# The dilated attention layer with its tokens ordered by residue modulo 4, and 64x64 class blocks for two of its three groups

## The chip, the core and the metric

The kernel runs on one core of one Trainium2 chip. The metric is the device time of one launch in microseconds (us): the kernel before takes 2082.92 us, the median of three runs (2081.38 to 2082.97). TensorE is called PE below, VectorE DVE, ScalarE ACT, GpSimd POOL, and SyncE, whose queue issues most DMA transfers, SP.

## The reference, cut to what matters

The program is a trunk of four layers on 256 tokens of width 1024, all in float32. Each layer has a token mixer, a cross-attention into 256 memory tokens and a squared-ReLU MLP. The mixer of layer 1, the second of the four, is a dilated attention with 16 heads of 64 features:

```
DIL_GROUPS = ((128, 1), (512, 4), (2048, 16))          # (window, dilation)
qkv = (x @ w_qkv).reshape(b, s, n_groups, 3, DIL_HEADS, DIL_HEAD_DIM)
# group (win, dil): query t attends to t, t-dil, ..., t-win (causal), with a T5 bias by distance
logits = q . k * 64**-0.5 + bias
o, lse = softmax(logits) @ v, log-sum-exp(logits)      # per group, per head
wts = softmax(stack(lses), axis=0)                      # over the three groups
o = einsum('gbsh,gbshe->bshe', wts, stack(outs)) @ w_out
x = layer_norm(alpha * x + o)
```

The mean over the groups, weighted by their softmax denominators, equals one softmax over the keys of all three groups together, and that is how both kernels compute it. With 256 tokens, a query of the second group (dilation 4) meets only keys of its own residue modulo 4, and one of the third group (dilation 16) only keys of its own residue modulo 16.

## The kernel before, in words

A large matrix product is split in two: each float32 operand becomes a rounded part `h` and a remainder `l`, and three products (h times h, h times l, l times h) add up in PSUM. `chunk` (lines 129 to 139) fetches 512 KB of a weight into one of 3 buffers `ws`; ACT casts it to `wh` (L137), DVE subtracts to get `wl` (L138); `wh` and `wl` have 9 buffers each. `xth` and `xtl` hold the tokens, transposed, with features on partitions (`to_xt`, which PE's transposes at L211, ACT's cast at L151 and DVE's subtraction at L152 make).

The dilated layer works by pairs of heads, 8 pairs. A query or key projection for one pair and one group is a unit `qk_unit` (L628, 24 matmuls of 256 columns, 6 such units to a pair); a value projection for four heads and one group is 48 matmuls of 256 columns (L193, 3 such units to two pairs). The first three value units have a planned order: token tile 0 of all three, then token tile 1 (`v_units`).

For each head, `scores` multiplies queries and keys in full float32, which PE runs as two passes for one instruction. For each of the three groups there is a 256-column product for query tile 1 (L677) and a 128-column one for query tile 0 (L679). `softmax` adds the bias and takes the maximum on DVE (L657), exponentiates on ACT (L663), and normalizes on DVE (L665), in two calls of 768 and 384 columns. Keys that the group's pattern leaves out have a bias of -1e30, so that all 256 or 128 keys of each group are worked on. `flip` transposes the nine 128x128 blocks of probabilities of a head (L692) and copies them from PSUM (L694). `values` multiplies them with the values of both heads of the pair (L704), each head to its own half of the output partitions. The bias comes from a table in DRAM (`dil_table`), read once per head into `hks` with one DMA (L672). At the end `project` multiplies with `w_out` (L169) and `norm` normalizes.

The order of the instructions on each engine is set by the program order of these functions and by a scheduler in the tile framework, which moves an instruction ahead of others of its engine when it expects its operands earlier. Semaphores wait at run time, and each engine works its own list in order. PSUM has 4 buffers `psA`, 2 `psB` and 2 `psT` of one bank each.

Of the kernel before, what the change touches and what calls it, by code (L numbers as in the profile page):

```python
# [11 lines left out]
F32 = mybir.dt.float32  # L12
# [7 lines left out]
P = 128  # L20
D = 1024
# [17 lines left out]
TW = 384  # L39
# [44 lines left out]
class Trunk:  # L84
# [70 lines left out]
    def gemm_tok(self, xt, t, ws, ps, k0=0, first=True, last=True):  # L155
# [6 lines left out]
        if last:  # L162
            steps = steps[:-TAIL] + [(k, (j,)) for j in every for k in range(n - TAIL, n)]
# [20 lines left out]
    def gemm_unit(self, xt, unit, ps, tiles=(0, 1)):  # L184
# [3 lines left out]
        for m in tiles:  # L188
# [25 lines left out]
    def to_xt(self, xt, src, t):  # L214
        xh, xl = xt
        for q in range(2):
            pt = self.transposes([src[:, (4 * q + i) * P:(4 * q + i + 1) * P] for i in range(4)])
            self.split(xh[:, 4 * q:4 * q + 4, t * P:(t + 1) * P], xl[:, 4 * q:4 * q + 4, t * P:(t + 1) * P],
                       pt.rearrange("p (a b) -> p a b", a=4))
# [31 lines left out]
    def norm(self, t, ps, gb, xt):  # L251
# [16 lines left out]
        if xt is not None:  # L268
            self.to_xt(xt, x, t)
# [114 lines left out]
    def mlp(self, layer, xt, xt_out):  # L384
# [46 lines left out]
        for t in range(NT):  # L431
            for u in range(NU - skew, NU):
                down(u, t)
            self.norm(t, acc[t], gb, xt_out)
# [154 lines left out]
    def dil_table(self, pool):  # L589


        nc, t_ = self.nc, self.t
        G = len(DIL)
# [3 lines left out]
        oh = self.sb.tile([P, G, TW], F32, name="onehot", tag="kt", bufs=2)  # L597
        nc.sync.dma_start(oh[:BUCKETS + 1], t_["rel_onehot"])
        tab = self.dr.tile([G, DH, TW], F32, name="reltab")
        for g in range(G):  # L600
            ps = self.T()
            nc.tensor.matmul(ps[:DH, :TW], rb, oh[:BUCKETS + 1, g, :], start=True, stop=True)
            sb = self.g2()
            nc.scalar.copy(out=sb[:DH, :TW], in_=ps[:DH, :TW])
            nc.sync.dma_start(tab[g], sb[:DH, :TW])
        return tab

    def dilated(self, layer, j, xt, xt_out):
        nc, v, t_ = self.nc, self.nc.vector, self.t
        G = len(DIL)  # L610
        gb = self.load_gb(layer, 0)
# [4 lines left out]
        hks = self.sb.tile([P, 2, 4, S], F32, name="hks", tag="kt", bufs=2)  # L616
        sbs = self.sb.tile([P, 2, 1024], F32, name="sbs", tag="vt", bufs=2)
        qk, vv, pr, pts = {}, {}, {}, {}
        oxt = self.xt()

        def qk_unit(hp, g, c):

            c0 = (g * 3 + c) * D + hp * P
            hi, lo = self.chunk(w[:, c0:c0 + P].rearrange("(k p) n -> p k n", p=P), (KC, P))
# [4 lines left out]
            o = qk[hp, g, c] = dp.tile([P, S], F32, name="qk", bufs=12)  # L629
# [5 lines left out]
        def v_units(hq, gs):  # L635

            us = [self.colunit(w, (g * 3 + 2) * D + hq * 256) for g in gs]
            ps = [self.A() if len(gs) > 1 else self.B() for _ in gs]
            for m in range(NT):
                for u, p_ in zip(us, ps):  # L640
                    self.gemm_unit(xt, u, p_, (m,))
            for g, p_ in zip(gs, ps):
                o = vv[hq, g] = dp.tile([P, NT, 256], F32, name="vv", bufs=5)
                nc.scalar.copy(out=o, in_=p_.rearrange("p (a b) -> p a b", a=2))

        def rev(hk, g0, n, top, w_):
            a = hk[:, g0:g0 + n, top:top + 1]
            return bass.AP(tensor=a.tensor, offset=a.offset,
                           ap=[list(a.ap[0]), [S, n], [-1, w_]])

        def softmax(sv, parts, n):

            mx = None
            o = 0
            for ps, bi, k in parts:
                m2 = self.sm.tile([P, 1], F32, name="dmx", tag="dmx", bufs=4)
                v.tensor_tensor_reduce(out=sv[:, o:o + k], in0=ps, in1=bi, scale=1.0,  # L657
# [671 lines left out]
```

## Time and profile before

| what | before |
|---|---|
| median of three runs | 2082.92 us (2081.38 to 2082.97) |
| the profiled execution's own time | 2083.81 us |
| its span, first to last instruction | 2082.0 us |
| mean granted clock of TensorE | 0.971 of full speed |
| PE busy | 1973.5 us (95% of the span) |
| DVE busy | 1314.8 us (63%) |
| ACT busy | 994.3 us (48%) |
| first value matmul of the dilated layer | 463.06 us |
| first scores of the layer | 509.23 us |
| scores of the last pair begin | 750.52 us |
| normalization of its first token tile begins | 774.16 us |

Times inside a run are counted from the first instruction. A row of the timeline gives start, length, engine, line, operation, output and inputs, shapes and count; what stands in brackets is the idle time of the engine before it and what ended it. A matmul's length is its latency, and successive ones overlap, so the distance from start to start is what one costs. In the chain of waits each row is a start, a length and the work that the end of the program hung on at that time.

### The profile page before, as it was taken

Reading aid. Unit: us, or ns where it says so; the run is one execution under the profiler, and the core shown is the slowest. Engines: PE = TensorE matmul, PEld = TensorE weight load, DVE = VectorE, ACT = ScalarE, POOL = GpSimd, SP = SyncE. Lnnn points to the kernel's source line nnn. Section 1 sums busy time; section 2 is a strip of 40 time slices with the busy share of each in tenths; the row PEclk is TensorE's granted clock in tenths of the full one; section 3 lists DMA queues with packets and bytes.
Section 4 is the critical chain, followed back from the end, with each engine's and each line's share of the span. In section 5 each row is a group of like instructions: output and inputs, shape, how many; then the busy total and the mean of one; then the engine's idle time right before and its main releaser. Section 6 shows DMA issues by size and latency. Waiting matters only on the chain.

```text
span 2082.0 us, 32815 instructions
## 1 busy us (share of the span) xinstructions
PE 1973.5 (95%) x12949; PEld 1744.4 (84%) x12949; DVE 1314.8 (63%) x2516; ACT 994.3 (48%) x1548; POOL 265.1 (13%) x160
## 2 busy tenths in 40 slices
PE   7999999999999999999999989989999898999998
PEld 7998789978989987798889878767898787877996
DVE  3986575464554557655486578776654499657554
ACT  4545455544444434365435543334655355545552
POOL 6960000000000000000021221100000663000000
PEclk8999999999999999999999989999999999999999
DMA  6644456657666625376646243334665441445762
GB/s 225 203 152 143 134 172 214 191 164 185 156 152 149 166 76 182 128 224 194 189 134 212 82 130 99 122 112 131 212 203 183 159 148 52 138 135 164 220 184 79
DMA packets 260409, 327.83 MB, mean 157 GB/s; under 512 B 25333, under 2 KB 220669, under 8 KB 260256
## 3 DMA queue, kind: packets, MB, share of 16 engines
q1 hardware_dynamic: 260256, 325.75, 51.6%
q8 instruction: 101, 1.65, 0.3%
q14 instruction: 52, 0.43, 0.1%
HBM read 318.81 MB, written 6.89 MB: 156 GB/s over the span
## 4 chain that ended last, share of the span: by engine, by line
PE 69%; DVE 15%; DMA 6%; ACT 4%; issue 4%; POOL 1%; SPq 0%; DVEq 0%; ACTq 0%; POOLq 0%
PE psA L169 24%; PE psB L181 20%; PE psB L628 6%; PE psB L193 5%; DVE g L519 3%; DVE wl L138 3%; PE psT L211 3%; ACT wh L137 2%; DMA ws<-in_m_w_dram 2%; PE psB L358 2%; PE psA L193 1%; PE psA L677 1%; DVE bnst L261 1%; DMA ws<-in_a_w_in_dram 1%; DVE psA L519 1%
## 5 line engine op out<-in xcount | busy, mean ns | idle before, releaser
L137 ACT CAST wh<-ws 128x1024 fp32r<-128x1024 f32 x546 | 571.3, 1050 | 709.3 <-PE psA L169 174.1
L138 DVE TENSOR_TENSOR wl<-ws,wh 128x1024 fp32r<-128x1024 f32 (+1 forms) x462 | 568.4, 1234 | 402.4 <-ACT wh L137 394.6
L181 PE MATMUL psB<-xth,wh 128*128 128x256 f32 x1280 | 369.4, 289 | 7.6 <-ACT xth L151 3.7
L181 PE MATMUL psB<-xth,wl 128*128 128x256 f32 x1280 | 367.3, 287 | 7.7 <-DVE wl L138 7.7
L181 PE MATMUL psB<-xtl,wh 128*128 128x256 f32 x1280 | 367.1, 287 | 0.0
L181 PEld LDWEIGHTS psB<-xth,wh 128*128 128x128 f32 x1280 | 250.2, 196 | 12.0 <-ACT xth L151 4.1
L138 POOL TENSOR_TENSOR wl<-ws,wh 128x1024 fp32r<-128x1024 f32 x84 | 211.1, 2536 | 376.8 <-ACT wh L137 364.1
L181 PEld LDWEIGHTS psB<-xth,wl 128*128 128x128 f32 x1280 | 250.0, 195 | 8.8 <-DVE wl L138 8.6
L181 PEld LDWEIGHTS psB<-xtl,wh 128*128 128x128 f32 x1280 | 250.0, 195 | 2.3 <-issue 0.2
L169 PE MATMUL psA<-wh,xth 128*128 128x512 f32 x512 | 185.8, 406 | 1.4 <-ACT xth L151 0.9
L169 PE MATMUL psA<-wl,xth 128*128 128x512 f32 x512 | 181.8, 399 | 0.0
L169 PE MATMUL psA<-wh,xtl 128*128 128x512 f32 x512 | 180.4, 398 | 0.0
L169 PE MATMUL psA<-wh,hth 128*128 128x512 f32 x512 | 163.7, 396 | 0.0
L169 PE MATMUL psA<-wh,htl 128*128 128x512 f32 x512 | 163.3, 395 | 0.0
L169 PE MATMUL psA<-wl,hth 128*128 128x512 f32 x512 | 162.2, 393 | 0.0
L519 DVE SCALAR_TENSOR_TENSOR psA<-chp,ccols,psA 128x256 f32<-128x256 f32 x280 | 119.1, 481 | 2.9 <-PE psA L503 0.4
L628 PE MATMUL psB<-xth,wh 128*128 128x256 f32 x384 | 112.6, 293 | 6.1 <-ACT qk L631 4.3
L169 PEld LDWEIGHTS psA<-wh,xth 128*128 128x128 f32 x512 | 97.7, 192 | 23.6 <-ACT xth L151 5.0
L169 PEld LDWEIGHTS psA<-wl,hth 128*128 128x128 f32 x512 | 96.5, 188 | 23.0
L169 PEld LDWEIGHTS psA<-wh,htl 128*128 128x128 f32 x512 | 96.2, 188 | 22.0
L828 POOL MEMSET rH<- 128x512 f32 x1 | 0.5, 526 | 894.6 <-DVE bnst L261 894.6
L169 PEld LDWEIGHTS psA<-wl,xth 128*128 128x128 f32 x512 | 97.5, 191 | 19.4
(321 smaller groups left out, 3612.5 us busy)
## 6 DMA issues: line engine op xcount, KB each, us to landing
ws<-in_m_w_dram SPq DMA_DIRECT2D x256, 512.0 KB, 4.0
ws<-in_b_w_qkv_dram SPq DMA_DIRECT2D x72, 512.0 KB, 3.9
ws<-in_x_w_kv_dram SPq DMA_DIRECT2D x64, 512.0 KB, 3.5
ws<-in_a_w_in_dram SPq DMA_DIRECT2D x32, 512.0 KB, 3.4
ws<-in_x_w_q_dram SPq DMA_DIRECT2D x32, 512.0 KB, 4.1
ws<-in_x_w_out_dram SPq DMA_DIRECT2D x32, 512.0 KB, 3.5
ws<-in_c_w_rkv_dram SPq DMA_DIRECT2D x24, 512.0 KB, 4.4
ws<-in_a_w_out_dram SPq DMA_DIRECT2D x16, 512.0 KB, 3.2
```

Of the source, the lines that this page charges most:

```text
L137: nc.scalar.copy(out=h[:rows], in_=f[:rows])
L138: self.lo_eng.tensor_tensor(l[:rows], f[:rows], h.bitcast(F32)[:rows], op=OP.subtract)
L169: nc.tensor.matmul(ps[j], l, r[:, j * 512:(j + 1) * 512], start=first and k == 0 and i == 0, stop=last and k == n - 1 and i == 2)
L181: nc.tensor.matmul(ps[:, c * S + toks.start:c * S + toks.stop], l, r, start=k == 0 and i == 0, stop=k == KC - 1 and i == 2)
L193: nc.tensor.matmul(ps[:, m * 256:(m + 1) * 256], l, r[:, k % 4, :], start=k == 0 and i == 0, stop=k == KC - 1 and i == 2)
L211: self.pe_last = self.nc.tensor.transpose(pt[:, i * P:(i + 1) * P], b, self.ident).ins
L261: v.bn_stats(st[:, j, :], xs)
L358: nc.tensor.matmul(op[:, c * S:(c + 1) * S], vt[:, m, (2 * h + c) * P:(2 * h + c + 1) * P], pT[:, m, :], start=m == 0, stop=m == 1)
L519: v.scalar_tensor_tensor(dst[:, o], hp[:, c, k:k + S], dwc(k, cc), src[:, o], op0=OP.mult, op1=OP.add)
L628: nc.tensor.matmul(ps, l[:, k, :], r[:, k, :], start=k == 0 and i == 0, stop=k == KC - 1 and i == 2)
L677: nc.tensor.matmul(s1[g // 2][:, (g % 2) * S:(g % 2 + 1) * S], q[g][r, P:], k[g][r, :], start=True, stop=True)
L828: nc.gpsimd.memset(H, 0.0)
```

## The change

The tokens of the dilated layer are put in a new order: by residue modulo 4, so that 64 tokens of class 0 come first, then class 1, 2 and 3. The MLP before the layer writes its transposed result in that order (`to_xt` with `classes`), and the layer's own output is written back in the old order (`back` in `values`), so that nothing else sees it.

In the second and third group a query then needs only the 64 keys of its own class. For each head and tile of 128 queries, which is two classes, `scores` now makes one product with all 256 keys for the first group and four products of 64x64 for the other two. A query's logits are 256 + 64 + 64 = 384 numbers in one PSUM bank, and one softmax of 384 columns per head and token tile takes the place of the calls of 768 and 384 columns per head. The third group's values and scores of odd classes are stored in the other half of the partitions, so that one transpose and one product with the values of 128 rows serve both groups: two small copies and two DMAs from ACT's queue per four heads arrange that (`v_unit`). Bias rows are read in four DMAs per pair in place of two.

The order of the work is new too. Weights are fetched up to three items ahead (`step`). The four softmaxes of a pair are issued one after each of the next pair's first four items, then its transposes and values. The last pair's softmaxes stand beside the first seven eighths of the output projection for token tile 0. The value units come one after the other, not by token tile.

```
-        oh = self.sb.tile([P, G, TW], F32, name="onehot", tag="kt", bufs=2)
+        oh = self.sb.tile([P, 1024], F32, name="onehot", tag="kt", bufs=2)
-        for g in range(G):
+        for g in range(2):
...
+            if classes:
+                o = [a[:, k, :].rearrange("p k (a i) -> p k a i", a=NC)[:, :, :, t * n:(t + 1) * n] for a in xt]
+                self.split(*o, pt.rearrange("p (k i a) -> p k a i", k=4, a=NC))
...
+        def v_unit(hq, g, unit):
+            ps = self.B()
+            self.gemm_unit(xt, unit, ps)
...
+            if g == 1:
+                for e in range(2):
+                    nc.scalar.copy(out=vs[hq][half(e), :, e, :], in_=ps[half(e)])
+            else:
+                o = dp.tile([P, NT, 256], F32, name="v2", bufs=1)
+                nc.scalar.copy(out=o, in_=ps)
+                for e in range(2):
+                    nc.scalar.dma_start(vs[hq][half(1 - e), :, e, :], o[half(e)])
...
+        def scores(hp):
+            hk = hks[:, hp % 2]
+            bias(hp + 1)
+            hs = (2 * hp, 2 * hp + 1)
+            ps = {(h, t): self.A() for h in hs for t in range(NT)}
+            for t in range(NT):
+                for h in hs:
+                    nc.tensor.matmul(ps[h, t][:, :S], qk[hp, 0, 0][row(h), t * P:(t + 1) * P], qk[hp, 0, 1][row(h), :],
+                                     start=True, stop=True)
+            for t in range(NT):
+                for b in range(2):
+                    for e in range(2):
+                        o = slice(t * P + SI * e, t * P + SI * e + SI)
+                        for h in hs:
+                            q, k = (qk[hp, 1 + (b ^ e), c] for c in range(2))
+                            nc.tensor.matmul(ps[h, t][half(e), S + SI * b:S + SI * b + SI], q[row(h), o], k[row(h), o],
+                                             start=True, stop=True)
+            def softmax(h, t):
...
+                v.tensor_tensor_reduce(out=sv[:, :S], in0=p_[:, :S], in1=along(b0, -1, (-NC, SI), NC), scale=1.0,
+                                       scalar=-3e38, op0=OP.add, op1=OP.max, accum_out=m1)
+                v.tensor_tensor_reduce(out=sv[:, S:S + X1], in0=p_[:, S:S + X1], in1=along(b1, 1, (-2, SI), 2), scale=1.0,
+                                       scalar=m1, op0=OP.add, op1=OP.max, accum_out=m2)
...
+        def flips():
+            for n in range(3):
+                if n < 2:
+                    src = [svs[:, n, t, b * P:(b + 1) * P] for b in range(2) for t in range(NT)]
+                else:
+                    src = [svs[:, h, t, S:S + X1] for h in range(2) for t in range(NT)]
+                pt = self.transposes(src)
+                o = self.g2()
+                (v.tensor_copy if n == 1 else nc.scalar.copy)(out=o, in_=pt)
...
+        def values(hp, pts, op):
+            *p0, p1 = pts
+            for b in range(2):
+                for h in hs:
+                    nc.tensor.matmul(op[row(h), :S], v0[h // 4][:, b, f(h)], p0[h % 2][:, b * S:(b + 1) * S],
+                                     start=b == 0, stop=False)
+            for a in range(NC):
+                for h in hs:
+                    o = slice(SI * a, SI * a + SI)
+                    nc.tensor.matmul(op[row(h), o], vs[h // 4][:, a // 2, a % 2, f(h)],
+                                     p1[:, h % 2 * S + SI * a:h % 2 * S + SI * a + SI], start=False, stop=a == NC - 1)
...
+        bias(0)
+        for _ in items(0):
+            step()
+        for hp in range(HP):
+            soft = scores(hp)
+            if hp < HP - 1:
+                for _ in items(hp + 1):
+                    step()
+                    if soft:
+                        soft.pop(0)()
+                values(hp, flips(), self.B())
+        wo = t_["b_w_out"][j]
+        ws = [self.rows(wo, k) for k in range(HP - 1)]
+        for f in soft:
+            f()
+        ps = [self.B(), self.B()]
+        self.gemm_tok(oxt, 0, ws, ps, last=False)
+        values(HP - 1, flips(), self.A())
```

In the changed kernel's own line numbers, L195 is the value units' matmul (L193 before), L213 the transpose (L211, and L692 for the probabilities), L648 the query and key units' (L628), L171 the projections with whole rows of a weight (L169), L611 the bias table's (L602). L710 is the scores of the first group, L718 the 64x64 blocks, L760 and L765 the values of the first and of the other groups.

On PE, at the start of the layer, this is the kernel before; x_81 and x_82 are token tiles 0 and 1:

```order
L211 MATMUL psT<-ident,x_81 128x128 x8
L193 MATMUL psA<-wh,xth 128x256
L193 MATMUL psA<-wl,xth 128x256
...
L193 MATMUL psA<-wh,xtl 128x256
L211 MATMUL psT<-ident,x_82 128x128 x4
L193 MATMUL psA<-wh,xth 128x256
L193 MATMUL psA<-wl,xth 128x256
L211 MATMUL psT<-ident,x_82 128x128 x4
...
L602 MATMUL psT<-onehot,relb 16x384 x3
```

The same place in the changed kernel:

```order
L213 MATMUL psT<-ident,x_81 128x128 x8
L213 MATMUL psT<-ident,x_82 128x128 x8
L195 MATMUL psB<-wh,xth 128x256
L195 MATMUL psB<-wl,xth 128x256
L195 MATMUL psB<-wh,xth 128x256
L611 MATMUL psT<-onehot,relb 16x512 x2
L195 MATMUL psB<-wh,xtl 128x256
```

Value matmuls stood between the transposes of the two token tiles before (47 of them ahead of the first transpose of tile 1); in the changed kernel none does.

Between the units of one pair and the next, PE has this in the changed kernel; the rows ahead are query and key units, those behind are value units, svs are the probabilities:

```order
L648 MATMUL psB<-xth,wl 128x256
L213 MATMUL psT<-ident,svs 128x128 x8
L710 MATMUL psA<-qk 128x256 x2
L213 MATMUL psT<-ident,svs 128x128 x4
L760 MATMUL psB<-g_5282,v_4682 64x256
L710 MATMUL psA<-qk 128x256
L760 MATMUL psB<-g_5289,v_4682 64x256
L760 MATMUL psB<-g_5282,v_4682 64x256
L760 MATMUL psB<-g_5289,v_4682 64x256
L765 MATMUL psB<-g_5296,vs 64x64 x8
L710 MATMUL psA<-qk 128x256
L718 MATMUL psA<-qk 64x64 x16
```

Before, the values of one pair were these rows, with the scores and the transposes of each head in other places between the units:

```order
L704 MATMUL psB<-g_5146,vv 64x256
L704 MATMUL psB<-g_5292,vv 64x256
L704 MATMUL psB<-g_5146,vv 64x128
L704 MATMUL psB<-g_5292,vv 64x128
L704 MATMUL psB<-g_5152,vv 64x256
L704 MATMUL psB<-g_5298,vv 64x256
```

All that is left of attention between two pairs' units now stands in one stretch, with the next pair's first scores between the transposes and the values.

## Rows read from the trace of the kernel before

**Rows 1.** The page, busy time of PE over the span.
```profile
PE 1973.5 (95%) x12949; PEld 1744.4 (84%) x12949; DVE 1314.8 (63%) x2516; ACT 994.3 (48%) x1548; POOL 265.1 (13%) x160
```

**Rows 2.** Windows: busy time by engine, from first scores to last pair's scores.
```profile
core 0: us, PE busy (x) PEld busy (x) DVE busy (x) ACT busy (x) POOL busy (x), PEclk, DMA share, GB/s
509.23:750.52 241.29, 236.15 (x1871) 221.28 (x1870) 128.46 (x260) 108.90 (x187) 0.00 (x0) 0.99 0.62 155
```

**Rows 3.** Chain of waits through the dilated layer.
```profile
464.97 5.64 PE psA L193 x41
...
472.56 2.12 PE psT L602 x6
...
541.59 2.10 PE psB L704 x24
...
546.75 1.49 PE psA L677 x6
548.24 0.67 PE psB L679 x6
...
551.97 0.66 PE psT L692 x6
...
558.89 5.76 PE psB L628 x48
...
750.52 1.06 PE psA L677 x4
...
766.83 7.31 PE psA L169 x31
774.16 0.70 DVE x L260
```

**Rows 4.** Timeline of PE, from the layer's start to its second stall.
```profile
461.73 1.61 PE L211 MATMUL psT<-ident,x 128*128 128x128 f32 x8 [3.80 <-DVE x L267]
463.06 0.58 PE L193 MATMUL psA<-wh,xth 128*128 128x256 f32 x1
...
470.45 0.60 PE L211 MATMUL psT<-ident,x 128*128 128x128 f32 x4
...
485.27 0.28 PE L628 MATMUL psB<-xth,wh 128*128 128x256 f32 x1
...
490.91 0.28 PE L628 MATMUL psB<-xth,wl 128*128 128x256 f32 x1
495.48 0.58 PE L628 MATMUL psB<-xth,wh 128*128 128x256 f32 x1 [4.29 <-ACT qk L631]
...
500.13 0.31 PE L628 MATMUL psB<-xth,wh 128*128 128x256 f32 x1
```

**Rows 5.** Timeline of ACT at that stall.
```profile
494.10 1.04 ACT L137 CAST wh<-ws 128x1024 fp32r<-128x1024 f32 x1 [0.43 <-DMA ws<-in_b_w_qkv_dram]
495.05 0.38 ACT L631 ACTIVATE qk<-psB 128x256 f32<-128x256 f32 x1
```

**Rows 6.** Timeline of PE: small matmuls of the third layer.
```profile
1151.68 0.49 PE L938 MATMUL psA<-rar,rbk 64*128 64x128 f32 x4
1152.10 0.44 PE L940 MATMUL psA<-rar,rbk 64*64 64x128 f32 x4
1152.46 0.49 PE L938 MATMUL psA<-rar,rbk 64*128 64x128 f32 x4
...
1276.03 1.15 PE L1043 MATMUL psA<-g,rW 128*64 128x64 f32 x32
...
1301.94 1.14 PE L1017 MATMUL psA<-rx,rW 64*64 64x64 f32 x16
```

**Rows 7.** Groups of DVE by line and shape, 604 to 678 us.
```profile
L138 DVE TENSOR_TENSOR wl<-ws,wh 128x1024 fp32r<-128x1024 f32 x19 | 23.2, 1223 | 20.7 <-ACT wh L137 20.6
...
L657 DVE CUSTOM_DVE_ANT_0 sbs<-psA,hks,dmx 128x256 f32<-128x256 f32 x4 | 1.9, 479 | 2.3 <-PE psA L677 2.3
L665 DVE TENSOR_SCALAR g<-g,dden 128x384 f32<-128x384 f32 x4 | 1.7, 418 | 0.1
```

More of the change, by code (lines that the diff above doesn't have):

```diff
@@ L38 @@
 REL_MAX = 2048
-TW = 384
+NC = 4
+SI = S // NC
 BIG = 1e30
@@ L162, in gemm_tok @@
         if last:
-            steps = steps[:-TAIL] + [(k, (j,)) for j in every for k in range(n - TAIL, n)]
+            m = max(n - TAIL, 0)
+            steps = steps[:m] + [(k, (j,)) for j in every for k in range(m, n)]
         for k, js in steps:
@@ L697, in values @@
-        def values(hp):
-            op = self.B()
-            for g in range(G):
-                for m, o, i in ((0, slice(0, S), slice(0, S)), (1, slice(P, S), slice(S, S + P))):
-                    for h in (2 * hp, 2 * hp + 1):
-                        ro = DE * (h % 2)
-                        hl = h % 4
-                        nc.tensor.matmul(op[ro:ro + DE, o], vv[h // 4, g][:, m, hl * DE:(hl + 1) * DE],
-                                         pts[h][g][:, i], start=g == 0 and m == 0, stop=g == G - 1 and m == 1)
-            self.split(oxt[0][:, hp, :], oxt[1][:, hp, :], op[:, :S])
@@ new lines, in run, with items, along @@
+        def run(item, chunks):
+            kind, i, g, c = item
+            if kind == "v":
+                v_unit(i, g, chunks)
+            else:
+                qk_unit(i, g, c, *chunks)
+        def items(hp):
+            if hp % 2 == 0:
+                yield from (("v", hp // 2, g, None) for g in range(G))
+            yield from (("qk", hp, g, c) for g in range(G) for c in range(2))
+        def along(a, step, n, m):
+            return bass.AP(tensor=a.tensor, offset=a.offset, ap=[list(a.ap[0]), [step, m], list(n)])
@@ new lines, in dilated, with step @@
+        todo = [i for hp in range(HP) for i in items(hp)]
+        ahead = []
+        def step():
+            while todo and len(ahead) < 3:
+                ahead.append((todo[0], prep(todo.pop(0))))
+            run(*ahead.pop(0))
+        bias(0)
[9 more added lines that the diff above has]
+                values(hp, flips(), self.B())
@@ new lines, in dilated @@
+        wo = t_["b_w_out"][j]
[5 more added lines that the diff above has]
+        values(HP - 1, flips(), self.A())
+        ws.append(self.rows(wo, HP - 1))
+        for t in range(NT):
+            if t == 0:
+                self.gemm_tok(oxt, 0, ws[-1:], ps, k0=HP - 1, first=False)
+            else:
+                ps = [self.A(), self.A()]
+                self.gemm_tok(oxt, 1, ws, ps)
+            self.norm(t, ps, gb, xt_out)
@@ L1292, in tile_trunk @@
                     fill = staged(2)
-                k.mlp(layer, xt, xo)
+                k.mlp(layer, xt, xo, nx is not None and nx % 3 == 1)
                 for _ in range(2 if nx == 2 else 0):
```

188 lines of the change are left out of this document (76 added, 112 removed).

## The prediction, as put on record

> **What bounds the kernel now.** I read the page first: PE is busy for 95% of the span [rows 1], so time is saved only where PE gets less to do or where it waits. Next the windows, for the stretch from the first scores to those of the last pair: 241.29 us, with PE busy for 236.15 and DVE and ACT for 128 and 109 [rows 2]. The reader is to see that this layer too hangs on PE, and that DVE and ACT have about half their time free; work on them is hidden as long as none of it comes just ahead of a PE instruction. The clock there is 0.99, so PE's costs can be read as distances from start to start. The chain of waits gives them: 48 unit matmuls of 256 columns in 5.76 us, 0.12 each [rows 3]. The stretch holds 42 query and key units (24 matmuls, 2.88 us each) and 9 value units (48, 5.76 us): 121.0 + 51.8 = 172.8 us, which the change leaves alone. The other 241.3 - 172.8 = 68.5 us are attention on PE and its waits, 9.8 us for each of 7 rounds (a round: the units of the next pair, then transposes, values and next scores). Last, the timeline of the layer's front shows what PE does before the first scores, and one long stall [rows 4].
>
> **The rounds.** What a pair costs on PE before, from the chain: scores 6 passes in 1.49 and 6 in 0.67, twice; 18 transposes at 0.66/6 = 0.11; 24 value passes in 2.10 [rows 3]. That is 4.3 + 2.0 + 2.1 = 8.4 of the 9.8 us; 1.4 are changes between shapes and waits.
>
> After, for a pair, counting two passes to each full-precision product:
> - Transposes: 12 at 0.11 = 1.3 us.
> - First group's scores: 8 passes of 256 columns. One head's passes cost 1.49/6 = 0.25 [rows 3]. The heads lie on different halves of the array's rows, and such a pair overlaps in the third layer: four passes of 128 columns have 0.49 us from first start to last end and make place for the next shape after 0.42, the one after that after another 0.36 [rows 6], where six one-headed ones take 0.67. As PE issues head 0 twice, then head 1 twice, I count three of every four passes, and both of a product that stands alone in the order: 0.75 + 0.5 + 0.5 = 1.75 us. Bounds: 0.95 (values' pace, below) and 2.0 (no overlap).
> - 64x64 blocks: 32 passes of 64 columns. In one quarter of the array 16 such take 1.14 us, 0.06 each after the latency of the last (0.22); on two halves in turn 32 take 1.15, 0.03 each [rows 6]. Bounds 1.0 and 2.0; I take 1.0, because successive products here always change halves too.
> - Values: 24 passes over 4608 columns in 2.10 us [rows 3] are 0.46 ns a column; 8 passes of 256 columns make 0.9 us. The 16 of 64 columns at 0.03 make 0.5 (bound 1.0).
> - Changes of shape: 8 in the row of instructions that replaces these pieces. L938 and L940 leave some 0.1 us each beyond their passes [rows 6]: 0.8 us, between 0.4 and 1.0.
>
> Sum 6.3 us, with bounds 5.1 and 8.2. Waits: the third set of transposes needs the first one's PSUM buffer copied, and the last values need the last copy; the next pair's scores that stand between give each copy over 1 us, so I add nothing, with 1.1 us as the upper bound if they give none. Seven rounds of 6.3 are 44 us in place of 68.5: 24.4 us less (33 and 3 at the bounds, 7 x 5.1 and 7 x 9.3 taken from 68.5).
>
> A rule of the Trainium skill speaks against small blocks: "TensorE: Matmul & The Clock Gate", section "Wait — 56ns, not 53.3ns?", says that with hardware decode off the sequencer spends about 62 ns on each matmul. By it the 48 short passes would cost 3.0 us and not 1.5, so 1.5 us more in each round and 2066 by it. The trace disagrees with its 0.03 us from start to start [rows 6], as far as two halves go.
>
> DVE in a round without value units: 6 remainders at 1.22 [rows 7], four softmaxes of at most 0.48 + 0.48 + 0.42 and small ones, some 1.7 each, copies 1.1: 15.2 of 23.6 us. ACT's exponentials shrink from 1152 to 768 columns a head. Both stay hidden; the weights that queue behind them are safe because the 9 buffers let casts run some 8 chunks (23 us of matmuls) ahead of use, where four softmaxes hold the queues for about 8 us. The same cover hides the added bias reads (8 transfers early in the layer, about the bytes of the two before) and the two transfers on ACT's queue, whose values are needed a whole pair later. If the cover went, each round would show a PE wait on `wl`.
>
> **The front.** Before, PE began the value units at 463.06 with token tile 0 alone, while DVE normalized tile 1, whose transposes came at 470.45 [rows 4]; the chain has 41 such matmuls ahead of them [rows 3]. In class order every tile of 128 tokens holds tokens of both halves, so no matmul can start before both are transposed, at about 472. All 9 units then come, 34.6 us, and the table: 2.12 us for 6 passes of 384 columns [rows 3], about 1.9 for 4 of 512. PE is cold by then: after the stall that ended at 495.48 it ran 22 matmuls until 500.13, 4.65 us in place of 2.64 [rows 4], so 2.0 us lost; I take the same here. End: 472 + 34.6 + 1.9 + 2.0 = 510.5, against 509.23.
>
> It is only 1.3 us later because I let the stall at 490.9 go (4.3 us of waiting and 2.0 of half clock). There the copy that frees a `psB` buffer stood in ACT's queue behind casts that waited for weights [rows 5], while the bias reads filled the transfers. After, that copy is due at about 495, not 488, with as many casts ahead of it, and the same weights have had 7 us more to land. If the stall stays, the front costs 6.3 us more.
>
> **The end.** Before, 23.6 us pass from 750.52, the last pair's scores, to 774.16, the normalization of tile 0 [rows 3]. After, the count goes from the first scores (2.4 us, all in one go), by 7 rounds, to the end of the last scores: 510.5 + 2.4 + 172.8 + 44.1 = 729.8. Then 42 output matmuls at 7.31/31 = 0.236 [rows 3], 9.9 us; beside them the last softmaxes take about 8 us, so PE hardly waits. Transposes and values 2.7, shapes 0.3 and waits for copies 0.7, the split of the result 1.2 (two operations of the size of the 0.42 one in [rows 7] and their hand-overs, an estimate), the last matmuls 0.9: 745.5. That is 28.7 us before 774.16, and from there on nothing differs. The profiled execution took 2083.8 us; 2083.8 - 28.7 = 2055.1, and its median counterpart is 0.9 lower: 2054 us.
>
> A second rule weighs on the end alone: "SBUF — State Buffer", section "Door 1: The DMA port swizzle (why `[64,N]` ≈ `[32,N]`)", says that every access in a new 16-byte line pays, and the new bias reads step by 16 bytes. No run here shows it; if the reads doubled (0.48 and 0.48 four times over), the last softmaxes would pass their cover by about 2 us, and the sum by it would be 2056.
>
> **Rivals.**
> - *The halves do not overlap, and copies are waited for.* First scores 2.0, blocks 2.0, short values 1.0, waits 1.1: 9.1 in place of 6.3 us, times 8 pairs 22 us: 2076. For it: L677 ran one head at a time, so no row has these very shapes in turn. Against it: L938 and L1043.
> - *The front keeps its stall.* Rounds as forecast, 6.3 us more: 2060. For it: the same weights pass the same 3 buffers, and the bias reads come ahead of the units. Against it: the later demand.
> - *Short passes go at the one-quarter pace, whatever halves they use:* something ahead of the array, such as the issue of matmuls, holds them at 0.06 us [rows 6], so 48 take 2.9 and not 1.5, 1.5 more for each of 8 pairs: 2066. L1017's row speaks for it; L1043's 0.03 against it. The rule quoted above names the sequencer as such a place.
> - *Slower: a pass costs the same whatever its width.* Before, a pair has 66 passes, transposes included, and 9.8 us: 0.148 each. After it has 76: 11.3 us. With 8 x 1.5 = 12 us and the front's 1.3, 2097. It decides above 0.13 us a pass, since 76 of these are 9.8 us. For it: latency, drains and weight loads come with each pass. Against it: in one and the same round 256 and 128 columns cost 0.25 and 0.11.
>
> **How the numbers follow.** Forecast 0.66, its own range 2046 to 2064 (rounds between 5.3 and 7.6 us). No overlap 0.16, front stall 0.08, slow short passes 0.03, slower 0.05, and 0.02 for something that eats the gain so that nothing is left. The range goes down to 2044, 10 us below the forecast, for rounds at their lower bound (8 x 1.2 us), and up to 2074, which takes in the front stall, the slow short passes and about half of the first rival: some 0.15 is left out. A measurement of this kernel tells 0.2%, 4 us, from no change; so faster 0.92, same 0.03, slower 0.05.
>
> **What would show it.** Rounds of 23.6 us without and 40.9 us with value units, start to start; L718's 32 passes in about 1 us and a `psA` row of L710 with overlap; no PE wait on ACT's `qk` copy near 491; the first value matmul at 472 and the first scores near 510; DVE and ACT without new waits ahead of PE. The prediction is wrong if a round exceeds 7.6 us beyond its units, if PE waits on `wl` or on the copies of the transposes, or if the first scores come after 517.

## The result, and the profile after

| what | before | after |
|---|---|---|
| median | 2082.24 us (2081.38 to 2082.97, 4 runs) | 2054.31 us (2050.32 to 2057.95, 4 runs) |
| ratio | 1 | 0.9866, interval 0.9842 to 0.9890 |
| ratio of a second series of 4 runs | 1 | 0.9894, interval 0.9878 to 0.9910 |
| profiled execution, its span | 2083.81, 2082.0 us | 2057.95, 2056.2 us |
| first scores | 509.23 us | 511.70 us (forecast 510.5) |
| last scores end | not compared: spread over heads | 732.26 us (forecast 729.8) |
| first normalization | 774.16 us | 747.14 us (forecast 745.5) |

The change makes the kernel 28 us faster, and the forecast of 2054 us holds. Below it, the steps hold in part: two waits of PE were taken as nothing, the copies of the transposes (0.27 us a round) and, behind the layer, where nothing was to differ, some 3 us.

The page, busy time of PE; it answers to [rows 1], 28.7 us less:

```profile
PE 1944.8 (95%) x13027; PEld 1716.0 (83%) x13027; DVE 1302.7 (63%) x2524; ACT 996.1 (48%) x1551; POOL 264.9 (13%) x160
```

Windows of after, from the first scores to the end of the last; it answers to [rows 2] (columns as there: bounds, length, busy PE, PEld, DVE, ACT, POOL, clock):

```profile
511.70:732.26 220.56, 218.67 (x2013) 203.11 (x2013) 121.63 (x272) 112.21 (x193) 0.00 (x0) 1.00 0.58 163
```

The reader is to see that PE is busy for 218.67 of 220.56 us. DVE and ACT are busy for 55 and 51% of it.

The chain of waits of after, for [rows 3]:

```profile
471.61 0.83 PE psB L195 x3
472.44 3.52 PE psT L611 x4
...
511.70 1.06 PE psA L710 x8
512.76 0.91 PE psA L718 x32
513.67 17.37 PE psB L648 x143
...
537.50 17.46 PE psB L195 x144
...
578.60 17.36 PE psB L648 x143
...
732.26 9.74 PE psB L171 x42
742.00 0.45 PE psT L213 x4
...
747.14 0.69 DVE x L269
```

From start to start, a round is 537.50 - 513.67 = 23.83 us without value units and 578.60 - 537.50 = 41.10 us with them (forecast 23.6 and 40.9). The units are 17.28 and 34.55 of that (144 or 288 matmuls at 0.12), so attention has 6.55 us per round, where 6.3 was forecast and 9.8 were spent before.

One round, by PE's timeline. What one row costs is the distance to the next:

```profile
572.08 1.04 PE L213 MATMUL psT<-ident,svs 128*128 128x128 f32 x8
573.04 0.70 PE L710 MATMUL psA<-qk 64*128 64x256 f32 x4
574.02 0.66 PE L213 MATMUL psT<-ident,svs 128*128 128x128 f32 x4 [0.27 <-ACT g L750]
574.61 0.65 PE L760 MATMUL psB<-g,v 128*64 128x256 f32 x2
575.18 0.70 PE L710 MATMUL psA<-qk 64*128 64x256 f32 x2
575.81 0.86 PE L760 MATMUL psB<-g,v 128*64 128x256 f32 x5
576.30 0.40 PE L765 MATMUL psB<-g,vs 128*64 128x64 f32 x4
576.51 0.38 PE L760 MATMUL psB<-g,v 128*64 128x256 f32 x1
576.72 0.63 PE L765 MATMUL psB<-g,vs 128*64 128x64 f32 x12
577.28 0.70 PE L710 MATMUL psA<-qk 64*128 64x256 f32 x2
577.90 0.69 PE L718 MATMUL psA<-qk 64*64 64x64 f32 x32
578.53 0.38 PE L648 MATMUL psB<-xth,wh 128*128 128x256 f32 x1
```

Added up by kind: transposes 0.96 + 0.59 = 1.55 us, L710 0.71 + 0.63 + 0.62 = 1.96, blocks 0.63, long values 1.27, short values 0.77, and one wait of 0.27 for the copy of the first transposes: 6.45 us between these two starts. The view of PE's waits from 511 to 745 us (us in total, times, longest) named copies of `qk` before, in front of scores and of units:

```profile
PE psA L677 <- ACT qk L633: 3.3, 3, 1.1
PE psB L628 <- ACT qk L633: 1.4, 3, 0.5
```

After has one kind left, on the copies of the transposes, and none on `wl`; seven of these waits stand in the seven rounds, the eighth in the layer's end:

```profile
PE psT L213 <- ACT g L750: 2.1, 8, 0.3
```

The front, by PE's timeline, for [rows 4]:

```profile
469.67 1.94 PE L213 MATMUL psT<-ident,x 128*128 128x128 f32 x8 [6.50 <-DVE x L276]
```

The clock of that stretch, in a window with the columns of [rows 2]:

```profile
461.70:479.10 17.40, 10.89 (x38) 6.73 (x36) 9.73 (x20) 3.49 (x6) 0.00 (x0) 0.51 0.57 161
```

The first value matmul comes at 471.61 us (forecast 472). PE is at its lower level here, 1.2 GHz (clock 0.51 from 461.70 to 479.10 us, 1.00 just before and behind). It fell just behind a wait of 3.81 us for the normalization of token tile 0; the wait of 6.50 us for tile 1 lies inside the stretch. Value matmuls stand 0.21 us apart until 479.03, and 0.12 behind it. The table falls into it. The stall of [rows 4] at 490.9 us is gone: the 144 matmuls from 494.42 us take 17.28 us without a wait.

Groups of DVE, 604 to 678 us, for [rows 7]:

```profile
L727 DVE CUSTOM_DVE_ANT_1 svs<-psA,hks 128x256 f32<-128x256 f32 x10 | 6.2, 624 | 0.0
...
L729 DVE CUSTOM_DVE_ANT_1 svs<-psA,hks,dmx 128x128 f32<-128x128 f32 x11 | 3.8, 346 | 0.1
...
L153 DVE TENSOR_TENSOR xtl<-psB,xth 128x256 fp32r<-128x256 f32 x2 | 1.2, 625 | 5.9 <-ACT xth L152 5.9
```

The bias read with 16-byte steps takes 0.624 us where 256 columns took 0.479 before. The engine has room for it.

### The profile page after: what moved, and what is told of

Same layout as the page of the kernel before. It is cut to its first block, busy times and chain, and to the rows that moved or that the text cites. A ratio compares the mean times of both kernels' runs of the same rounds, so it can differ in the third digit from the quotient of the medians.

```text
span 2056.2 us, 33010 instructions
## 1 busy us (share of the span) xinstructions
PE 1944.8 (95%) x13027; PEld 1716.0 (83%) x13027; DVE 1302.7 (63%) x2524; ACT 996.1 (48%) x1551; POOL 264.9 (13%) x160
## 3 DMA queue, kind: packets, MB, share of 16 engines
q10 hardware_dynamic: 1152, 1.05, 0.2%
## 4 chain that ended last, share of the span: by engine, by line
PE 68%; DVE 15%; DMA 6%; ACT 5%; issue 4%; POOL 1%; SPq 0%; DVEq 0%; ACTq 0%; POOLq 0%
PE psA L171 25%; PE psB L183 19%; PE psB L648 7%; PE psB L195 6%; DVE g L528 3%; DVE wl L139 3%; PE psT L213 3%; ACT wh L138 2%; DMA ws<-in_m_w_dram 2%; PE psB L367 2%; POOL wl L139 1%; DMA ws<-in_x_w_out_dram 1%; DVE x L269 1%; DVE bnst L270 1%; DMA ws<-in_x_w_kv_dram 1%
## 5 line engine op out<-in xcount | busy, mean ns | idle before, releaser
L183 PE MATMUL psB<-xth,wh 128*128 128x256 f32 x1280 | 369.1, 289 | 9.4 <-ACT xth L152 3.7
L171 PE MATMUL psA<-wh,xth 128*128 128x512 f32 x496 | 180.2, 406 | 3.5 <-ACT xth L152 3.0
L171 PE MATMUL psA<-wl,xth 128*128 128x512 f32 x496 | 177.1, 400 | 0.0
L171 PE MATMUL psA<-wh,xtl 128*128 128x512 f32 x496 | 175.9, 399 | 0.0
L171 PE MATMUL psA<-wh,hth 128*128 128x512 f32 x512 | 163.7, 396 | 0.0
L171 PE MATMUL psA<-wh,htl 128*128 128x512 f32 x512 | 163.3, 395 | 0.0
L171 PE MATMUL psA<-wl,hth 128*128 128x512 f32 x512 | 162.3, 393 | 0.0
L171 PEld LDWEIGHTS psA<-wh,xth 128*128 128x128 f32 x496 | 94.8, 193 | 25.2 <-ACT xth L152 7.1
L171 PEld LDWEIGHTS psA<-wl,hth 128*128 128x128 f32 x512 | 96.5, 188 | 22.9
L171 PEld LDWEIGHTS psA<-wh,htl 128*128 128x128 f32 x512 | 96.2, 188 | 22.0
L171 PEld LDWEIGHTS psA<-wl,xth 128*128 128x128 f32 x496 | 94.9, 192 | 19.0
L171 PEld LDWEIGHTS psA<-wh,xtl 128*128 128x128 f32 x496 | 94.6, 191 | 18.9 <-DVE xtl L153 0.2
```

What stands on the lines that cost most here:

```text
L171: nc.tensor.matmul(ps[j], l, r[:, j * 512:(j + 1) * 512], start=first and k == 0 and i == 0, stop=last and k == n - 1 and i == 2)
L183: nc.tensor.matmul(ps[:, c * S + toks.start:c * S + toks.stop], l, r, start=k == 0 and i == 0, stop=k == KC - 1 and i == 2)
```

## The experiments

Stage times are read from each profile, because the totals of one program spread by up to 15 us between executions (e_end: 2054.77 to 2069.79). "Layer" below is the time from the first scores to the first normalization: 264.93 us before, 235.44 after.

**e_again.** No edit.

> The changed kernel once more, nothing edited, to see how far two profiled executions of one program differ. Theory: the dilated layer repeats to 0.2 us (a round without value units 23.8 us, one with them 41.1 us, norm tile 0 at 747 us), and what differs between executions lies in the stages behind it, in the cross-attention, where the first profile lost 5 us; total 2051 to 2058 us. Rival: the layer's own short products make the spread, and rounds differ by 0.5 us or more from one profile to the other.

Measured: 2056.16 us (2053.40 to 2060.60). Six rounds repeat within 0.1 us (23.82, 41.09); one with value units took 41.85, where the chain shows PE behind a cast that had waited for its weights. The layer took 236.16 us. The two differ by more behind the cross-attention, not in it as I had expected (from normalization to normalization it takes 267.10 us in after and 267.57 in e_again). The layer that follows, in windows of after and of e_again, between the same two normalizations:

```profile
1024.00:1341.50 317.50, 292.55 (x2539) 254.53 (x2538) 230.85 (x647) 148.67 (x324) 61.88 (x62) 0.95 0.42 129
```
```profile
1025.00:1337.80 312.80, 287.81 (x2540) 250.31 (x2538) 231.11 (x646) 148.70 (x324) 61.99 (x62) 0.97 0.43 131
```

The work is the same, the granted clock is 0.95 against 0.97, and all 4.7 us of difference are in PE's busy time. So most of what these two executions differ by comes from a stage that the change does not touch. The rival is right for one round of seven, which lost 0.75 us.

**e_blocks2.** Each block product twice.

```
-                        for h in hs:
+                        for h in hs + hs:
```

> Each 64x64 product of the class blocks is issued twice (the second writes the same values again). Theory: the four quarters run beside each other and 32 passes take 0.62 us, so 32 more take about as long: rounds of 24.4 and 41.7 us, +0.6 us for each of 8 rounds, 2059 us (2057 to 2062). Rival: a pass costs what a full-height pass costs, 0.148 us: +4.7 us a round, rounds of 28.5 and 45.8 us, 2092 us.

Measured: 2064.09 us (2058.19 to 2067.78); rounds of 24.34 and 41.62 us (541.14, 582.76 and 607.10 in its chain), +0.51. PE's timeline of one round:

```profile
581.55 1.21 PE L718 MATMUL psA<-qk 64*64 64x64 f32 x64
582.69 0.38 PE L648 MATMUL psB<-xth,wh 128*128 128x256 f32 x1
```

64 passes take 1.14 us, 32 took 0.63: an added pass costs 0.016 us, a ninth of the rival's 0.148. That refutes the slower rival for these blocks. The 8 x 0.51 = 4 us are in the layer (239.56 us). The median is 8 us above e_again's and past the 2062 us expected at most; what exceeds the 4 us is not in this layer.

**e_heads.** The heads one after the other.

```
-            for t in range(NT):
-                for h in hs:
+            for h in hs:
+                for t in range(NT):
```

(and so in the loop over the blocks)

> The score products run head by head instead of alternating between the two heads (the same products, another order), in the full-width part and in the class blocks. Theory: two products that lie in different halves of TensorE's rows run beside each other only when they are neighbours in the order; head by head the 8 full-width passes take 2.0 us in place of 1.06 and the 32 block passes about 1.2 in place of 0.62, a round +0.8 to 1.5 us, total about 2062 us (2058 to 2068). Rival: the halves do not overlap and a pass is just short: no row changes, the same time within 0.2%.

Measured: 2063.68 us (2061.92 to 2064.48); rounds 24.18 and 41.47, +0.35, where +0.8 to 1.5 were expected; the layer 238.34 us. The first go is a miss: its 8 passes take 1.07 us in this order too, as long as one head's four alone take below, so the second head's ran beside them. In a round, where pieces are short, the halves show:

```profile
572.76 1.13 PE L710 MATMUL psA<-qk 64*128 64x256 f32 x4
573.82 0.66 PE L213 MATMUL psT<-ident,svs 128*128 128x128 f32 x4
...
577.71 0.98 PE L718 MATMUL psA<-qk 64*64 64x64 f32 x32
```

Four passes of one head take 1.06 us (0.27 each, the pace of L677 in [rows 3]), four of two heads 0.71; 32 blocks 0.90 and 0.63. The sum of +0.6 is +0.35 in the round because the wait for the copy (0.27) has gone: the longer scores cover it. The median lies in the expected range, 7.5 us above e_again's, but only some 3 us of that are in the layer, so the mechanism does not account for the total.

**e_dve2.** Two more multiplications per softmax.

```
+                v.tensor_scalar(sv[:, :S + X1], sv[:, :S + X1], 1.0, None, op0=OP.mult)
+                v.tensor_scalar(sv[:, :S + X1], sv[:, :S + X1], 1.0, None, op0=OP.mult)
```

> Two more passes of VectorE over the 384 score columns in each softmax (times 1.0), some 0.4 us each, 8 more in a round: +3.4 us of VectorE per round. Theory: VectorE stands beside TensorE's units in a round and has slack, and the last softmaxes end 3.7 us before TensorE comes to their transposes: rounds within 0.3 us of 23.8 and 41.1, total +0 to +1 us. Rival: the softmax is now on the path: +3.4 us a round, +27 us, 2081 us.

Measured: 2055.53 us (2053.89 to 2064.05). Rounds are 23.83 and 41.10 as before, but for one pair of rounds that is 1.0 longer. The chain there goes through casts that waited for weights, as in e_again, but here it also goes through the added multiplications of two softmaxes, with a weight cast behind them on ACT. The window from first to last scores:

```profile
513.15:734.70 221.55, 218.91 (x2014) 203.15 (x2013) 134.40 (x328) 112.26 (x193) 0.00 (x0) 1.00 0.58 162
```

DVE's busy time grew by 12.8 us (less than the 27 I had counted), PE's by 0.2. In the other five rounds DVE is hidden. Whether the added work cost the 1.0 us is open: e_again and e_table lose 0.75 and 1.0 us in one round without it.

**e_ahead1.** Prefetch of one unit, not three.

```
-            while todo and len(ahead) < 3:
+            while todo and len(ahead) < 1:
```

> Only one unit's weights are loaded ahead in place of three. Theory: the lead is set by the buffers that hold the cast weights, and TensorE's order is the same: rounds of 23.8 and 41.1 us within 0.3, total within 2 us. Rival: with shorter attention between the units TensorE comes to the next weights sooner than before, and with less lead it waits for the casts: rounds longer by several us, total +10 us or more.

Measured: 2060.73 us (2055.65 to 2061.98); rounds 23.82 and 41.10, the layer 235.53 us. The depth of `ahead` carries no time in this layer. The median is 4.6 us above e_again's, more than the 2 us expected; no row of the layer shows where.

**e_end.** The last softmaxes and values ahead of the whole output projection.

```
-        ps = [self.B(), self.B()]
-        self.gemm_tok(oxt, 0, ws, ps, last=False)
...
-            if t == 0:
-                self.gemm_tok(oxt, 0, ws[-1:], ps, k0=HP - 1, first=False)
-            else:
-                ps = [self.A(), self.A()]
-                self.gemm_tok(oxt, 1, ws, ps)
+            ps = [self.A(), self.A()]
+            self.gemm_tok(oxt, t, ws, ps)
```

> Undoes the order at the end of the layer: the last two units' softmaxes and values stand ahead of the whole output projection, none of whose matmuls covers them. Theory: TensorE then waits for the last softmaxes, done at 738.3 us, 6.0 us behind the last scores, and norm tile 0 starts some 6 us later, near 753 us; total +5 to +8 us, 2060 us. Rival: the softmaxes' chain is hidden anyway or norm tile 0 waits for something else: within 1 us.

Measured: 2059.95 us (2054.77 to 2069.79); the layer 241.38 us, +5.9. PE's waits, 725 to 760 us:

```profile
PE psT L213 <- DVE dnm L733: 3.3, 1, 3.3
```

With two shorter kinds (0.8 and 0.7) it is 4.8 us of waiting, and then slower matmuls for a while. So at the layer's first normalization the new end is worth 6 us, as forecast. In the profiles half of it is gone by the end of the cross-attention, which is 3.2 us shorter here than in after (see "Behind the layer" below); the totals of the two overlap.

**e_full128.** The blocks as whole products.

```
-                            nc.tensor.matmul(ps[h, t][half(e), S + SI * b:S + SI * b + SI], q[row(h), o], k[row(h), o],
+                        nc.tensor.matmul(ps[h, t][:, S + P * b:S + P * b + P], q[row(h), o], k[row(h), o],
```

> The class blocks of the second and third group are computed as whole products of 128 x 128 for each token tile and group (16 passes of 128 columns in two halves of TensorE's rows, in place of 32 of 64 columns in four quarters); the softmax still reads 128 columns, which are then the wrong ones. Theory: four quarters run beside each other and two halves do not make up for it: 16 passes at 0.055 to 0.07 us take 0.9 to 1.1 us in place of 0.62: rounds +0.3 to 0.5, total +2 to +4 us. Rival: a pass costs the same whatever its width, so 16 passes cost half of 32: rounds 0.3 us shorter.

Measured: 2056.90 us (2054.30 to 2061.28); rounds 24.09 and 41.38, +0.27; in the first go the 16 passes take 1.16 us, 32 blocks 0.91. Four quarters do beat two halves, by 2 us in the layer: a small part of the gain.

**e_stride.** Contiguous steps.

```
-                v.tensor_tensor_reduce(out=sv[:, :S], in0=p_[:, :S], in1=along(b0, -1, (-NC, SI), NC), scale=1.0,
+                v.tensor_tensor_reduce(out=sv[:, :S], in0=p_[:, :S], in1=hk[:, h % 2, :S].rearrange("p (a b) -> p a b", a=NC), scale=1.0,
...
-            back = lambda x: x.rearrange("p (i a) -> p a i", a=NC)
+            back = lambda x: x.rearrange("p (a i) -> p a i", a=NC)
```

> The bias is read with a contiguous step in place of steps of 8 and 16 bytes and the result of a pair is written in contiguous order (left out: the right order of the bias and of the layer's output tokens). Theory: the strided steps made VectorE's and ScalarE's rows longer, and without them L727 goes from 0.62 to about 0.45 us, L153's split from 0.62 to 0.42 and L152's from 0.61 to 0.37; hidden in the rounds (within 0.1 us), 0.4 us earlier at norm tile 0, total within the noise. Rival: the 256-column rows are longer for another reason (the new instruction form), and stay at 0.6.

Measured: 2055.72 us (2053.87 to 2058.51), rounds unchanged, the layer 235.21 us. Groups of DVE, 604 to 678 us:

```profile
L727 DVE CUSTOM_DVE_ANT_0 svs<-psA,hks 128x256 f32<-128x256 f32 x10 | 4.2, 419 | 0.4 <-PE psA L718 0.4
L729 DVE CUSTOM_DVE_ANT_0 svs<-psA,hks,dmx 128x128 f32<-128x128 f32 x11 | 3.8, 346 | 0.1
...
L153 DVE TENSOR_TENSOR xtl<-psB,xth 128x256 fp32r<-128x256 f32 x2 | 0.8, 424 | 5.5 <-ACT xth L152 5.5
```

Where the step was 16 bytes, 0.624 becomes 0.419 and 0.625 becomes 0.424 (ACT's split L152: 0.614 to 0.372). L729, with steps of 8 bytes and the same change of form, keeps 0.346: the step made the price, not the form.

**e_table and e_warm.** The table behind the MLP's last products; e_warm adds 24 unused products there.

```
+            if classes and t == NT - 1:
+                self.tab = self.dil_table()
+                wm = self.B()
+                for _ in range(WARM):
+                    nc.tensor.matmul(wm[:, :P], self.ident, self.x[0][:, :P], start=True, stop=True)
```

> The products that make the bias table are issued behind the last down-projection matmuls of the MLP ahead of this layer, where TensorE waits for the norm, in place of between the first value matmuls. Theory: the table cost 3.5 us of TensorE's path at the half clock; the first scores come at 508.2 us in place of 511.7, everything behind them as early, total about 3.5 us less (2048 to 2053 us). Rival: the table filled a wait for the second tile's transposes or weights that now stands empty: first scores and total within 1 us of the changed kernel's.

> As with the table moved, and 24 full-precision products of 128 columns more (their result is not used) in the same wait of TensorE, so that it is not idle there. Theory: the half clock from 461.9 to 479.1 us follows that idle stretch; with it filled, part of the 17 us runs at the full clock: first scores near 506.3 us, total about 5.5 us less than the changed kernel (2046 to 2051 us). Rival: the half clock starts from something else, or the filler delays the transposes behind it by as much as it gains: first scores at or behind 508.2 us.

Measured: 2053.25 us (2050.99 to 2059.93) and 2057.97 us (2054.48 to 2065.41). In e_table PE's timeline has the table ahead of tile 1's transposes:

```profile
467.22 3.59 PE L614 MATMUL psT<-onehot,relb 33*16 33x512 f32 x4 [1.27 <-DVE xtl L154]
471.25 1.94 PE L214 MATMUL psT<-ident,x 128*128 128x128 f32 x8 [0.44 <-DVE x L277]
```

From those transposes to the first scores it takes 509.64 - 471.25 = 38.39 us, in after 511.70 - 469.67 = 42.03: the forecast's 3.5 us and no more. The first scores come at 509.64 us, not 508.2, because tile 1 was normalized 1.6 us later in this execution. One later round took 1.0 us longer (its wait for the copy of the transposes was 1.3 us, not 0.3), so the layer's end keeps 2.6 of the gain. In e_warm the window from 462.00 to 479.10 has a clock of 0.90, where after had 0.51, but the first scores come at 508.30, not 506.3:

```profile
465.31 1.93 PE L618 MATMUL psT<-onehot,relb 33*16 33x512 f32 x4
467.17 4.96 PE L449 MATMUL psB<-x,ident 128*128 128x128 f32 x42
471.96 1.04 PE L215 MATMUL psT<-ident,x 128*128 128x128 f32 x8
```

Tile 1 was normalized by 469.9 us (DVE's row begins at 468.45 and lasts 1.42), and the filler ran until 471.96: it gave back 2 us of what it gained. In the totals neither kernel differs from after.

**e_group and e_best.** The piece shapes of the round above suggested another order.

```
-        for hp in range(HP):
-            soft = scores(hp)
-            if hp < HP - 1:
...
-                values(hp, flips(), self.B())
+        soft = scores(0)
+        for hp in range(HP - 1):
...
+            pts = flips()
+            soft = scores(hp + 1)
+            values(hp, pts, self.B())
```

e_best writes `pts = flips((0, 1))` and `values(hp, pts + flips((2,)), self.B())`, and has e_warm's edit with 12 products.

> The next pair's scores are written ahead of this pair's values, so that on TensorE the score products stand in pieces of 4, 4 and 32 passes ahead of the value products and not in pieces of 4, 2, 2 and 32 between them. Theory: in the changed kernel's rounds each change of shape costs time (L710 x2 takes 0.63 us, 8 in one go 1.06), and the softmax that follows is no sooner needed: attention per round goes from 6.55 to about 5.4 us (L710 0.7 + 0.6, L718 0.8, values in one go 1.4, transposes 1.55 and 0.27 of wait), rounds of 22.7 and 40.0 us, 7 x 1.1 = 8 us less in all, 2047 us. Rival: the pieces between are covers for the copies of the transposes, and what grouping saves comes back as waits of TensorE on those copies: rounds of 23.5 us or more.

> The order of the grouped kernel, with the third set of transposes behind the scores (one piece of 8 full-width passes and 32 block passes between the two sets of transposes), the bias table moved to TensorE's wait ahead of the layer, and 12 unused full-precision products there. Theory: no wait for the copy (0.27 us), scores 1.06 + 0.9, transposes 1.55, values 1.4: attention per round 4.9 us, rounds of 22.2 and 39.5 us; the filler ends before the second tile is normalized, at 469.2 us, so the first scores come at 505.4 us (511.7 in the changed kernel): 7 x 1.65 + 6.3 = 18 us less, 2038 us (2034 to 2044). Rival: rounds stay at 23.5 us or more through waits on copies, or the front stays at 508 us, as with 24 products: 2047 us or more.

Measured: e_group 2048.36 us (2043.10 to 2051.42), ratio 0.9844 (0.9817 to 0.9871), rounds 22.64 and 39.92; e_best 2046.34 us (2042.06 to 2050.70), ratio 0.9837 (0.9810 to 0.9863), rounds 22.10 to 22.16 and 39.38. The chain of e_best, one round:

```profile
588.81 0.87 PE psT L215 x8
589.68 1.06 PE psA L717 x8
...
593.44 17.47 PE psB L197 x144
```

Attention in the round is 593.44 - 588.81 = 4.63 us against 6.45, with no wait: 1.06 for L710 in one piece (L717 here) where three pieces took 1.96. The rounds come out as forecast. The total of 2038 us does not, and the front is the largest part of the miss:

```profile
463.50 3.59 PE L618 MATMUL psT<-onehot,relb 33*16 33x512 f32 x4
467.02 4.21 PE L449 MATMUL psB<-x,ident 128*128 128x128 f32 x18
471.02 1.76 PE L215 MATMUL psT<-ident,x 128*128 128x128 f32 x8
```

Here 18 passes took 4.0 us, 0.22 each, where e_warm's took 0.114: this time they ran at the lower level. The number of fillers did not decide it. Up to the table PE did the same in both, eight transposes and six filler passes behind a wait of 4.88 us, and the table then took 1.93 us in e_warm and 3.59 in e_best (clock 1.00 in e_warm from 466 us on, 0.50 in e_best until 472). First scores 507.83 us, in an execution whose normalization ahead of the layer came 2.2 us earlier than after's, so 1.7 us gained where 6.3 were forecast. At the end e_best gives back 1.0 us of wait: the pair's split result (`xtl`) stands on DVE behind the next pair's softmaxes. Layer: e_group 228.05, e_best 224.91 us, against 235.44. Both beat the changed kernel by 7 to 9 us in the median (e_stride of the same series, with after's rounds, had 2055.72); that e_best beats e_group is not shown by totals, only by its rounds.

## Why the prediction came out right

**The round** was sized 6.3 and is 6.55 us, through errors that cancel. Blocks: 1.0 forecast, 0.63 measured; four quarters overlap further than the two halves of [rows 6]. L710: 1.75 forecast, 1.96 measured. I had counted its pieces of 4, 2 and 2 passes as the order has them; the four fit (0.75 forecast, 0.71 measured), and a pair standing alone costs 0.63, not 0.5. Long values 0.9 against 1.27, cut up too; short ones 0.5 against 0.77; transposes 1.3 against 1.55. These four are 1.1 us above their sizes and the blocks 0.4 below; the difference is about the 0.8 set aside for changes of shape, which is inside the measured sums. So what makes the round longer than forecast is mainly the wait. Taken as nothing, it is 0.27: the copy that should have been covered stands on ACT behind a cast (1.05) and the last `qk` copy (0.27). A wait on the copies of the transposes was one of the signs by which the prediction called itself wrong, and by that sign this step failed: the next pair's scores that stand in between, 0.71 us, do not cover the copy. It costs 1.9 us in seven rounds, too little to move the total out of its range.

The seven rounds hold 45.9 us of attention, where 68.5 were spent before. By the view of waits, 2.8 us of these 22.7 are waits that are gone. How the rest splits between fewer columns and the new order of the work is not shown: no run has the class order with the old order of work.

**Rivals.** That the halves do not overlap fails by the 0.71 us of four passes and by e_heads; a price per pass whatever the width fails by e_blocks2 (its 2097 us start from the profiled execution; from the median they are 2096). Slow short passes fail too: 0.016 to 0.02 us for a block pass and, in one piece, 0.03 for a short value pass (L772 in e_best, 16 in 0.47 us), not 0.06. The 62 ns for each matmul that the Trainium skill gives for hardware decode off ("TensorE: Matmul & The Clock Gate", "Wait — 56ns, not 53.3ns?") therefore did not bind these passes. No run here shows whether that decode was on.

**The front** is 2.5 us later than before, where I had 1.3. The step that was mis-sized is the table: 1.9 us forecast, 3.52 measured, since I priced it at the full clock and set the half-clock loss (2.0) beside it as a separate term; the table ran inside the half-clock stretch. e_table shows it as the table's own 3.5 us. The 2.0 us for the value matmuls fit: 144 of them take 19.3 us at first (0.83 + 18.45), and 17.28 at the full clock. The stall's going is as forecast.

**The end.** From the end of the last scores to the first normalization 747.14 - 732.26 = 14.9 us (15.7 forecast): the last softmaxes are done at 738.3 us, 3.7 us ahead of the transposes at 742.00. e_end shows what this cover is worth. The Trainium skill's rule on 16-byte lines ("SBUF — State Buffer", "Door 1: The DMA port swizzle (why `[64,N]` ≈ `[32,N]`)") is borne out in kind: such steps cost 1.47 to 1.65 times the contiguous ones in e_stride. It did not reach PE, because that slack takes it up: the 2 us feared did not come.

**Behind the layer** I had said that nothing differs, and this step failed. At the first normalization after is 27.0 us ahead, at the end of the cross-attention (1017.1 us, 1040.6 before) 23.5. PE waits 8.8 us in this stretch, 5.6 before. The largest new wait is at its start, on PE's timeline of after:

```profile
762.77 1.22 PE L171 MATMUL psA<-wh,xth 128*128 128x512 f32 x2 [1.67 <-ACT xth L152]
```

ACT's timeline there, in after:

```profile
761.19 1.04 ACT L138 CAST wh<-ws 128x1024 fp32r<-128x1024 f32 x1 [0.82 <-PE psT L213]
762.14 1.06 ACT L152 CAST xth<-psT 128x512 fp32r<-128x512 f32 x2
```

And in before, where PE did not wait for `xth`:

```profile
785.18 0.59 ACT L151 CAST xth<-psT 128x512 fp32r<-128x512 f32 x1 [0.58 <-PE psT L211]
```

In after the `xth` casts stand on ACT behind a weight cast that came late (in e_again the same cast waited 0.98 us for its transfer). The order on ACT is another one, though the change does not edit this part: between the first normalization and the first `xth` cast ACT has seven weight casts in after and four before. The transfers of the weights did not start later: behind the normalization the first was issued at 750.88 us, 780.04 before. e_end, with the old end of the layer, has four casts again and no such wait, and from normalization to normalization it takes 263.95 us, before 263.57, after 267.10. The other eleven runs, all with the new end, have seven casts, this wait of 0.9 to 2.0 us, and 265.8 to 269.0 us. So the new end of the layer brings another order of ACT behind it, and that goes with the loss. The wait on `xth` is about half of the 3.5 us; what the other waits come from is not shown. That the median still met the forecast is in part luck: the profiled execution gained 25.9 us, two others of the four 31 and 32 (against the median before), and e_again's series is 22.7 us below its own before.

What stays open is what decides between the two levels of the clock in the front (e_warm 0.90, e_best 0.67 from 460.20 to 479.10 us) and in the later stages.

## What to carry to other kernels

Price a group of short matmuls by its pieces in the order as built: full-precision products of two heads overlap when they stand together, and the same eight passes cost 1.06 us in one piece and 1.96 in three. Where a scheduler cuts such groups up, writing the next scores ahead of the values in the program was worth another 1.2 us a round, and 1.7 with the last transposes behind the scores. And look at the order of every engine behind the stage that was changed, too: here ACT's order in the next stage had become another one without an edit there, and 3.5 us of 27 went in that stage.

## What the runs showed of the hardware that was not expected

64x64 products on four quarters of the array cost 0.02 us a pass (32 in 0.63 us), and a second set of 32 only 0.016 us each. A 16-byte step between float32 elements made the rows of DVE and ACT 1.5 to 1.65 times longer over 256 columns (0.624 against 0.419 us, 0.614 against 0.372); an 8-byte step over 128 columns cost nothing (0.346 both times). With an idle stretch filled by matmuls, the granted clock of the front was 0.90 in one execution and 0.67 in another, though PE had done the same until the clock rose in the first.
